# Reordering a branch's channels so that its passes through DRAM are wide transfers, and spreading the first loads over three queues

## The chip, the cores and the metric

One Trainium2 chip, all eight NeuronCores. Each core computes one sequence of the batch and the cores exchange nothing. The metric is the device time of the slowest core in microseconds (us). In some executions, of any kernel, one die (cores 0 to 3 or 4 to 7) or both show a lower granted TensorE clock and take longer; such runs are left out.

## The reference, cut to what matters

```python
D_MODEL, BATCH, SEQ, N_META = 2048, 8, 2048, 16       # 16 meta tokens in front: L = 2064
E_CONV = E_SSM = 1024; CONV_WIDTH = 31; SSM_GROUP = 16; SSM_STATE = 64

def reference(x, meta, norm_g, w_in, ...):
    h = jnp.concatenate([broadcast(meta), x], axis=1)
    xn = _rmsnorm(h, norm_g)
    proj = jnp.einsum("bld,de->ble", xn, w_in)         # v, g, z_c, u, z_s: 1024 columns each;
    v_c, g_c, z_c, u_s, z_s, gl_c, gl_s = split(proj)  # gl_c, gl_s: 2048 each
    y_c = _conformer_conv(v_c, g_c, z_c, ...)   # v*sigmoid(g), causal conv over 31 frames, LN, silu, *silu(z)
    y_s = gelu(_s5_scan(u_s, ...))              # diagonal state space, 64 groups of 16 channels
    y_s = y_s * sigmoid(y_s @ w_glu + b_glu)
    y_s = y_s * silu(z_s)
    merged = sigmoid(gl_c + b) * (y_c @ w_conv) + sigmoid(gl_s + b) * (y_s @ w_ssm)
    h = h + merged @ w_out
    return _rmsnorm(h, final_g)[:, N_META:, :]          # float32, (8, 2048, 2048)
```

## The kernel before

The kernel is a list of operations (each with engine, estimated duration, what it reads and writes, and a priority). A planner, written in Python and run when the kernel is built, simulates the five engines and the DMA and fixes **one order of instructions for each engine**. On the chip every engine runs its list in that order and waits on semaphores, whatever is ready behind. The planner's model of a DMA is this:

```python
    def schedule(self, bw=280e3):                 # bytes per us
        # ... cut: always take the ready operation of highest priority on the engine that is free first
            if o.dsrc is not None:                # a DMA: all share one pipe of 280 GB/s
                start = max(end, dma_free)
                dma_free = start + o.nbytes / bw
                end = dma_free + 2.2
            else:
                end += 0.2
            self.order[e].append(o)
```

Time is split in 8 phases j of NC = 258 frames. The input comes transposed in four quarters for each phase, all on the SP queue. It is squared and summed (ACT, DVE), summed over partitions by PE, normalised by square root and reciprocal, and scaled into XM, the right-hand operand of all projections:

```python
        def x_load(j):
            for q in range(4):
                t, b = XQ[j % 3][q]                                   # three chunk buffers of 4 quarters
                xl[j, q] = dma("sp", [(t, x_t[j][:, q * 4 * NC:(q + 1) * 4 * NC])], ..., prio=1)
        def x_chunk(j):
            # ... cut: Square, adds, matmul with ones
            act(r_, ps[bk][:, 0:NC], AF.Sqrt, bias=NORM_EPS, scale=1.0 / D, ...)
            xrc[j] = recip(r_, r_, NC, (rB,), (rB,), prio=2)
            # ... cut: 16 scalings into XM
```

Then come the u projections, 1024 matmuls of 258 columns, in waves as chunks arrive. Each result is copied by ACT to one of six small buffers ("pieces") and stored to DRAM. The scratch tensor is there because the state-space part needs another layout: PE produces 128 channels on the partitions, the scan wants partition = (phase j, channel h of its group) and the 8 groups g side by side. Before the change the DRAM tensor keeps a whole row of 2064 frames for each channel:

```python
    u_scr = scratch("u_scr", [8, 128, L])                             # row of 4128 bytes per channel
            cp("act", pt[:, 0:NC], ps[bk][:, 0:NC], ...)              # PSUM -> piece
            dma("sp", [(u_scr[m][:, lo:lo + NC], pt[:, 0:NC])], ...)  # 128 rows of 516 bytes, 4128 bytes apart
            # ... later, in the state-space part:
            us = u_scr[m].rearrange("(g h) (j c) -> j h g c", h=16, j=8)
            dma("sp", [(u3[16 * j:16 * j + 16, :, :], us[j]) for j in range(8)], ...)   # 8 narrow loads
```

The tensor a (v times sigmoid of g, on its way to the convolution), y (scan output) and c (convolution output) go the same way. The v and g projections that follow u run over five tiles of 412 or 414 columns (V_TILES).

## Time and profile before

| | before |
|---|---|
| time, median of 3 (lowest to highest) | 1682.75 us (1682.45 to 1683.12) |
| span by core in the profiled run | 1671.1 to 1683.8 us |
| PE work at full clock, a core with a complete record | 1609.7 us |
| PE time lost, mean of six cores | 56.2 us, 55.5 of it in the first 225 us |
| last quarter of the input lands | 106 to 114 us |
| last u matmul starts | 184 to 191 us |

The page of the profile, slowest core: the span, the busy tenths of PE in 40 slices of 42 us, the granted TensorE clock in tenths, the DMA packets, and the shares of the chain of waits that ended last.

```profile
span 1683.8 us, 23977 instructions; the slowest of 8 cores (1671.1 to 1683.8 us)
...
PE   3689899999999999999999999999999999999997
...
PEclk6899999999999999999999999999999999999999
...
DMA packets 129572, 200.70 MB, mean 119 GB/s; under 512 B 22576, under 2 KB 85296, under 8 KB 127280
...
PE 90%; DMA 5%; DVE 3%; issue 2%; ACT 0%; SPq 0%; DVEq 0%; ACTq 0%; POOL 0%; POOLq 0%
```

PE is full from the sixth slice on, at full clock. Only the first slices, and a little the fifth, have room.

The PE timeline of the same core: start, duration, line, operation, count; in brackets the idle time before it and what ended it. L605 is the matmul that sums a chunk's squares, L343 a projection.

```profile
26.94 2.06 PE L605 MATMUL ps<-CY,ST 128*128 128x258 f32 x4 [16.98 <-DVE CY L317]
34.55 1.02 PE L343 MATMUL ps<-XM,WS 128*128 128x258 bf16 x4 [5.56 <-DVE XM L328]
...
182.75 7.20 PE L343 MATMUL ps<-XM,WS 128*128 128x258 bf16 x64
189.79 5.76 PE L343 MATMUL ps<-XM,ST 128*128 128x414 bf16 x32
199.99 20.32 PE L343 MATMUL ps<-XM,ST 128*128 128x414 bf16 x101 [4.43 <-ACT ST L333]
```

The first projection stands at 34.55 us, the last 64 u matmuls end at 189.8 us, and after 32 more matmuls PE waits 4.43 us for a copy out of PSUM.

Waits of PE, from the table of waits (total us, times, longest):

```profile
PE ps L605 <- DVE CY L317: 25.0, 3, 17.0
...
PE ps L343 <- DVE XM L328: 12.0, 5, 5.6
PE ps L343 <- ACT ST L333: 10.8, 8, 4.4
```

### The profile page before, as it was taken

How to read it: one execution, taken by the hardware profiler on the slowest of the kernel's cores; microseconds unless marked ns; L12 is line 12 of the kernel's file. 1: busy time of each engine (PE TensorE's matmuls, PEld its weight loads, DVE VectorE, ACT ScalarE, POOL GpSimd, SP SyncE). 2: the span in 40 equal slices, each digit the busy share in tenths (PEclk: the TensorE clock that was granted, in tenths of full speed). 3: DMA queues.
4: the chain of work that ended last, by engine and by line, in shares of the span. 5: the costliest groups of instructions: out<-in, count | busy, mean ns of one | idle time of the engine just before them, and what ended most of it. 6: DMA issues, size and time to landing. Idle time of an engine off the chain costs nothing.

```text
span 1683.8 us, 23977 instructions; the slowest of 8 cores (1671.1 to 1683.8 us)
## 1 busy us (share of the span) xinstructions
PE 1615.7 (96%) x8565; PEld 841.5 (50%) x8650; DVE 725.3 (43%) x1254; ACT 522.5 (31%) x890; POOL 108.0 (6%) x220
## 2 busy tenths in 40 slices
PE   3689899999999999999999999999999999999997
PEld 2568666666655544444444444444444444444443
DVE  4978327867656826267322111111111122225433
ACT  2645214445345589344111111111111111122221
POOL 1000100000000000001010000000101100100000
PEclk6899999999999999999999999999999999999999
DMA  9972856777767873325764444445655653936612
GB/s 217 208 153 56 128 109 115 129 132 140 128 118 143 189 219 76 88 82 105 147 105 76 76 76 75 76 76 88 99 89 89 101 91 84 179 108 235 215 76 75
DMA packets 129572, 200.70 MB, mean 119 GB/s; under 512 B 22576, under 2 KB 85296, under 8 KB 127280
## 3 DMA queue, kind: packets, MB, share of 16 engines
q0 software_dynamic: 33792, 92.29, 35.8%
q1 hardware_dynamic: 95664, 106.88, 23.5%
q8 instruction: 71, 1.16, 0.3%
q14 instruction: 45, 0.37, 0.1%
HBM read 248.89 MB, written 42.50 MB: 173 GB/s over the span
## 4 chain that ended last, share of the span: by engine, by line
PE 90%; DMA 5%; DVE 3%; issue 2%; ACT 0%; SPq 0%; DVEq 0%; ACTq 0%; POOL 0%; POOLq 0%
PE ps L343 89%; DMA u_scr<-ST 2%; DVE CY L317 1%; DMA SM<-par 1%; DMA WS<-w_dw 1%; DMA CY<-x_t 1%; DVE XM L328 1%; PE ps L605 0%; DMA CY<-par_b 0%; SPq L355 0%; DVE ST L337 0%; DVE CY L328 0%; PE ps L349 0%; ACT ST L333 0%; PE ps L344 0%
## 5 line engine op out<-in xcount | busy, mean ns | idle before, releaser
L343 PE MATMUL ps<-XM,WS 128*128 128x512 bf16 (+3 forms) x5216 | 1013.4, 351 | 18.4 <-DVE XM L328 12.0
L343 PEld LDWEIGHTS ps<-XM,WS 128*128 128x128 bf16 x5216 | 511.3, 98 | 471.5 <-issue 24.1
L310 ACT ACTIVATE ST<-ps,SM 128x512 f32<-128x512 f32 (+2 forms) x224 | 135.7, 625 | 620.7 <-PE ps L343 589.7
L328 DVE SCALAR_TENSOR_TENSOR ST<-ps,ST 128x512 f32<-128x512 f32 x132 | 91.2, 691 | 507.1 <-PE ps L343 498.0
L343 PE MATMUL ps<-CY,WS 128*128 128x512 bf16 x1218 | 282.0, 379 | 3.3
L343 PEld LDWEIGHTS ps<-CY,WS 128*128 128x128 bf16 x1280 | 125.2, 98 | 151.0
L317 DVE TENSOR_TENSOR CY<-CY 128x257 f32<-128x257 f32 (+3 forms) x192 | 125.5, 669 | 31.5 <-ACT CY L310 14.2
L310 ACT ACTIVATE ST<-ps 128x512 bf16<-128x512 f32 (+3 forms) x112 | 61.2, 551 | 180.0 <-PE ps L343 176.8
L310 ACT ACTIVATE CY<-CY 128x514 f32<-128x514 f32 (+2 forms) x104 | 87.7, 861 | 66.5 <-DVE CY L317 30.4
L317 DVE TENSOR_TENSOR CY<-ps,CY 128x514 f32<-128x514 f32 (+1 forms) x96 | 65.1, 685 | 93.4 <-PE ps L343 88.9
L355 POOL DMA_DIRECT2D WS<-w_main x102 | 54.3, 532 | 594.8 <-PE ps L343 546.6
L343 PE MATMUL ps<-XM,ST 128*128 128x512 bf16 (+2 forms) x411 | 85.9, 371 | 4.7 <-ACT ST L333 4.4
L317 DVE TENSOR_TENSOR CY<-CY,ST 128x128 f32<-128x128 f32 (+3 forms) x112 | 62.2, 590 | 39.1 <-DMA CY<-par_b 19.4
L317 DVE TENSOR_TENSOR ST<-ST 128x512 f32<-128x512 f32 (+3 forms) x87 | 55.0, 647 | 33.5 <-ACT ST L947 28.7
L343 PEld LDWEIGHTS ps<-XM,ST 128*128 128x128 bf16 x416 | 41.4, 100 | 48.8 <-issue 7.7
L333 ACT CAST ST<-ps 128x258 bf16<-128x258 f32 (+1 forms) x96 | 41.4, 442 | 70.4 <-PE ps L343 56.2
L343 PE MATMUL ps<-XM 128*128 128x512 bf16 x251 | 56.3, 379 | 0.3
L343 PE MATMUL ps<-CY,XM 128*128 128x512 bf16 x251 | 56.3, 379 | 0.3
L343 PE MATMUL ps<-CY,ST 128*128 128x512 bf16 x251 | 55.2, 379 | 0.3
L328 DVE SCALAR_TENSOR_TENSOR XM<-CY,SM,ST 128x258 bf16<-128x258 f32 x128 | 51.6, 480 | 0.3
L343 PE MATMUL ps<-CY 128*128 128x256 bf16 (+1 forms) x320 | 50.6, 272 | 0.0
L328 DVE SCALAR_TENSOR_TENSOR ST<-ST,ps 128x412 bf16<-128x412 f32 (+1 forms) x40 | 23.3, 584 | 60.6 <-PE ps L343 39.3
(81 smaller groups left out, 809.2 us busy)
## 6 DMA issues: line engine op xcount, KB each, us to landing
WS<-w_main POOLq DMA_DIRECT2D x102, 512.0 KB, 8.2
CY<-x_t SPq DMA_DIRECT2D x32, 516.0 KB, 13.2
WS<-w_br POOLq DMA_DIRECT2D x32, 512.0 KB, 6.7
WS<-w_dw POOLq DMA_DIRECT2D x32, 320.0 KB, 7.2
z_scr<-ST SPq DMA_DIRECT2D x64, 128.0 KB, 3.9
ST<-z_scr SPq DMA_DIRECT2D x32, 256.0 KB, 3.4
WS<-x SPq DMA_DIRECT2D x8, 1024.0 KB, 6.9
CY<-x SPq DMA_DIRECT2D x8, 1024.0 KB, 12.8
```

What stands on the lines that cost most here:

```text
L310: f = lambda e: e.activation(out=out_, in_=in_, func=func, bias=bias, scale=scale)
L317: return S.op(eng, lambda e: e.tensor_tensor(out=out_, in0=in0, in1=in1, op=op), d, reads, writes, **kw)
L328: return S.op("dve", lambda e: e.scalar_tensor_tensor(out=out_, in0=in0, scalar=scalar, in1=in1, op0=op0, op1=op1), 0.15 + n / 960.0, read ...
L333: return S.op("act", lambda e: e.copy(out=out_, in_=in_), 0.22 + n / 1200.0, reads, writes, **kw)
L343: return lambda e: e.matmul(a[0], a[1], a[2], start=a[3], stop=a[4])
L355: return lambda e: e.dma_start(out=o, in_=i, allow_slow_non_contiguous=True)
```

## The change

The intent: permute the channels of each group of 128 on the host (weights, biases), so that the wanted layout in DRAM has long runs, and each of the eight narrow transfers per tile becomes one transfer with rows of 4 KB on one side; start earlier by loading the first chunk over two queues, weights and later chunks over a third; replace square root and reciprocal with Ln and Exp on ACT. The diff also changes the planner's DMA model and makes the v, g and convolution weight loads wait for an earlier tile.

```diff
-    def schedule(self, bw=280e3):
+    def schedule(self, bw=320e3):
-                start = max(end, dma_free)
-                dma_free = start + o.nbytes / bw
-                end = dma_free + 2.2
+                now, left = max(end, ring[e]), float(o.nbytes)
+                others = sorted(v for q, v in ring.items() if q != e and v > now)
+                while True:                      # each queue its own pipe; they share 320 GB/s
+                    rate = min(bw / (1 + len(others)), 0.78 * bw)
+                    # ... cut
+                ring[e] = end = now + left / rate
+                end += 2.2
# ... cut
-    u_scr = scratch("u_scr", [8, 128, L])
-    a_scr = scratch("a_scr", [8, 128, L])
-    y_scr = scratch("y_scr", [8, 128, SEQ])
-    c_scr = scratch("c_scr", [8, 128, SEQ])
+    u_scr = scratch("u_scr", [8, 8, 128, NC])
+    a_scr = scratch("a_scr", [8, 8, 128, NC + 2])
+    y_scr = scratch("y_scr", [8, 8, 128, NR])
+    c_scr = scratch("c_scr", [8, 8, 128, NR])
# ... cut: the input loads
+                eng = ("act" if q % 2 else "sp") if j == 0 else "sp" if j < 3 else "pool"
+                xl[j, q] = dma(eng, [(t, x_t[j][:, q * 4 * NC:(q + 1) * 4 * NC])], ...,
+                               prio=0 if j == 0 else 1 + j / 10, after=...)
# ... cut: the power tables of the scan move behind chunk 3; the small parameters load later
-            act(r_, ps[bk][:, 0:NC], AF.Sqrt, bias=NORM_EPS, scale=1.0 / D, ...)
-            xrc[j] = recip(r_, r_, NC, (rB,), (rB,), prio=2)
+            act(r_, ps[bk][:, 0:NC], AF.Ln, bias=NORM_EPS, scale=1.0 / D, ...)
+            xsq[j] = act(r_, r_, AF.Exp, scale=-0.5, ...)
# ... cut: v and g in 8 tiles of 258 (5 of 412 before), eleven piece buffers of 520 bytes (6 of 1024)
-            pi, pt, pB = piece()
-            dma("sp", [(u_scr[m][:, lo:lo + NC], pt[:, 0:NC])], ...)
+            pi, pt, pB = chunk_piece()
+            dma("sp", [(u_scr[m][j], pt[:, 2:NC + 2])], ...)      # 128 rows of 516 bytes, touching
# ... cut
-            us = u_scr[m].rearrange("(g h) (j c) -> j h g c", h=16, j=8)
-            dma("sp", [(u3[16 * j:16 * j + 16, :, :], us[j]) for j in range(8)], ...)
+            dma("sp", [(u2, u_scr[m].rearrange("j (h g) c -> (j h) (g c)", g=8))], ...)
# ... cut: a the same; y and c one wide store each, and a narrow read in one issue
# ... cut: the swap of halves by matmul becomes two ACT copies
+    sw = np.arange(E).reshape(8, 8, 16).transpose(0, 2, 1).reshape(-1)     # on the host
+    for a in range(0, 5 * E, E):
+        w_in[:, a:a + E] = w_in[:, a + sw]
+    w_conv, w_ssm, w_glu = p["w_conv"][sw], p["w_ssm"][sw], p["w_glu"][sw][:, sw]
```

## The prediction

> **What bounds it now.** TensorE: the page gives PE 96% busy, the chain of waits is 90% PE. By stage (table of windows, slowest core) it is 98-100% busy at granted clock 1.00 from 210 us to its last matmul at 1673 us. Only the first 200 us have room: PE 13.5, 29.2 and 35.4 us busy in the first three 42 us windows, clock 0.67, 0.80, 0.92. In the PE timeline the first projection stands at 34.6 us; the first 1024 matmuls (128x258, 110.8 ns each back to back: 208 in 23.04 us) end at 189.8 us, for 113.5 us of work. Then comes a 4.4 us wait for a copy out of PSUM (behind a store of narrow pieces, 16.6 us in the chain) and a cold restart (128 matmuls in 25.0 us, 174 ns each when warm: 2.7 us lost). The warm times of all matmuls after 200 us leave under 8 us of loss there, plus a 10 us tail. So relief of DMA, SP, DVE or ACT after 200 us is worth nothing.
>
> **What the change does.**
> 1. Wide transfers: u and a reads go from 1024 packets of 516 B (28 ns each) to 128 of 4128 B (160 ns), 1.8 to 1.3 us per tile on 16 engines, and 7 of 8 issues vanish (0.4-0.5 us of SP each). For y and c the narrow side only moves from write to read. All under a saturated PE: about 0.
> 2. Start. The first chunk's loads get two queues, and no competition from three early weight loads and later chunks. The Trainium skill (DMA: Bandwidth & Descriptors, Issuing engines are not separate DMA queues) says that more queues save only issue time; I count the ordering, not bandwidth. The small parameter load now lands at 24 us (20.5 us in the chain), holding DVE; afterwards earlier. Estimate from 300 GB/s seen here: first projection near 22 us.
> 3. Chunk chain: the reciprocal (1.77 us, DVE, x8) becomes Ln and Exp on ACT (about 0.4 each; the skill's ScalarE: Activation LUTs, Table sets, has both in one set, so no 1.28 us reload per chunk). DVE, 40.5 of 42 us busy from 42 to 84 us, then needs 10.6 us per chunk, not 12.4; the power tables (about 9 us) move behind chunk 3. Chunks come every 12 us, not 14-15.
> 4. Eleven piece buffers for six: most waits for copies (10.8 us in the table of waits) go.
> 5. PE work: v/g tiles of 258 for 412: 2048x110.8 - 1280x174.1 ns = +4.1 us. Swap matmuls to ACT: 16x0.215 = -3.4 us.
>
> **Sum.** Steps 2-4: projections end near 153 us, not 190: -37. Gap and cold restart: -7. PE work: +0.7. Narrow tiles with three banks leave 3.5 us, not 5.6, for emptying a bank: +3 of new stalls. About -40 us: **1643 us**, range 1627 to 1663. Chances: faster by over 2% 0.62, within 2% 0.37, slower 0.01.
>
> **What would show it.** First projection at 20-26 us; last u matmul at 145-162 us; no 4 us gap after; no table load between Ln and Exp; PE still 99-100% from 210 us; some 11,000 DMA packets fewer without effect after 200 us.
>
> **What would make it wrong.** Loads of chunks 3-7 stuck behind weight loads on the POOL queue; all cores loading at once, chunks slower than 12 us; table reloads per chunk (+2.6 us each); the static instruction order, planned with faster DMA, making PE wait in order; narrow v/g tiles stalling over 5 us; or the start shrinking more than I think (limit about -60 us).

## More of the kernel before

Kernels are compared by executions in the undisturbed state.

Near the middle comes the gate stage: 32 gate matmuls, then the two branch matmuls of 8 each, for 64 blocks. The second branch, the state-space one, needs YS already multiplied by z, in 16 multiplications on DVE, the z tiles coming back from DRAM through three buffers:

```python
            if n % 2:
                for m in range(8):
                    z_, zB = z_load(m, h, 4)                          # 128x1024, from DRAM, 3 buffers
                    tt(ys, ys, z_, ALU.mult, n=1024, ...)
        # ... gate stage, for each block: gates, then
                    for br_, (sv, sB) in enumerate(((CBv, CBq), (YSv, YSq))):
                        proj(b3[:, br_ * 8:br_ * 8 + 8, :], brB, 0, lambda k: sv[:, k, n * 512:(n + 1) * 512], ...)
```

"PE time lost" is my own sum over the trace: for each matmul, the time from its start to the next matmul's start, less what a matmul of that width takes when nothing holds it. For that I use columns / 2.4 + 2.5 ns, which fits the distance of starts that the trace shows back to back (110 ns at 258 columns, 174 ns at 412, 216 ns at 512, core 1); a matmul of 4-byte numbers counts four times. The sum counts waits and the cold clock after them. Two of the eight cores miss some 85 matmul records in each trace and are left out.

The gate stage in the PE timeline of core 1 (whose matmul records are complete):

```profile
788.97 7.07 PE L343 MATMUL ps<-XM,WS 128*128 128x512 bf16 x32
795.88 1.89 PE L343 MATMUL ps<-CY,WS 128*128 128x512 bf16 x8
...
806.24 7.07 PE L343 MATMUL ps<-XM,WS 128*128 128x512 bf16 x32
813.14 7.07 PE L343 MATMUL ps<-CY,WS 128*128 128x512 bf16 x32
```

The last matmul of the preceding stage (GLU) starts at 788.8 us. PE then runs three blocks of 32 gate matmuls with two conv products between them before it comes to the state-space products at 813.14, 24.4 us later. The last of the DVE multiplications they need (the ninth in DVE's list, eight for this half and one for the next) had ended at 808.5 us, 19.7 us after that GLU matmul:

```profile
807.82 0.69 DVE L317 TENSOR_TENSOR CY<-CY,ST 128x1024 bf16<-128x1024 bf16 x1 [2.80 <-DMA ST<-z_scr]
```

The order planned has some 5 us to spare here, and nothing waits.

## The result

The changed kernel is correct and takes 1703.7 us in the median of 4 runs (1701.48 to 1705.5), against 1682.93 us (1682.45 to 1684.09) for the kernel before. The ratio is 1.0122 with a 95% interval of 1.0104 to 1.0139: 1.2% slower, where 2.4% faster was predicted. A ratio here is always the mean time of one kernel's fast runs over that of the other's fast runs of the same rounds, so not quite the ratio of the medians quoted. The calls ran on several chips, and the kernel before took 1682.9 to 1686.5 us in them, so between calls 2 or 3 us mean nothing.

The page after, the same lines:

```profile
span 1701.6 us, 25563 instructions; the slowest of 8 cores (1688.3 to 1701.6 us)
...
PE   4789999999999999997999999999999999999997
...
PEclk7899999999999999998999999999999999999999
...
DMA packets 115114, 200.85 MB, mean 118 GB/s; under 512 B 19376, under 2 KB 68784, under 8 KB 112816
...
PE 85%; DMA 10%; DVE 2%; ACT 1%; issue 1%; SPq 1%; POOL 0%; DVEq 0%; ACTq 0%; POOLq 0%
```

Packets fell by 14,458 (129,572 to 115,114). The DMA share of the chain rose from 5% to 10%, and slice 19 (766 to 808 us), where PE was full before, falls to 7 with the clock at 8.

The PE timeline of the slowest core (L619 sums squares, L350 is a projection):

```profile
20.82 2.06 PE L619 MATMUL ps<-CY,ST 128*128 128x258 f32 x4 [10.76 <-DVE CY L324]
25.80 1.02 PE L350 MATMUL ps<-XM,WS 128*128 128x258 bf16 x4 [2.92 <-DVE XM L335]
...
173.31 7.21 PE L350 MATMUL ps<-XM,WS 128*128 128x258 bf16 x64
180.37 3.68 PE L350 MATMUL ps<-XM,ST 128*128 128x258 bf16 x32
185.96 0.61 PE L356 MATMUL ps<-ident,CY 128*128 128x128 bf16 x8 [1.91 <-DVE CY L324]
```

The start came as predicted: the first projection at 25.80 us for 34.55, and no 4 us gap when u ends. But the last 64 u matmuls start at 173.3 us and end at 180.4 us, 10 us earlier than before, not 37.

The waits of PE:

```profile
PE ps L350 <- DVE CY L324: 16.0, 1, 16.0
...
PE ps L350 <- ACT ST L340: 13.3, 5, 4.5
...
PE ps L619 <- DVE CY L324: 10.8, 1, 10.8
...
PE ps L350 <- DVE XM L335: 9.2, 2, 6.3
```

Waits for copies (ACT, L340) did not go; they are 13.3 us, where they were 10.8. And there is a wait of 16 us that did not exist before. It stands in the gate stage, here on core 1:

```profile
785.69 7.07 PE L350 MATMUL ps<-XM,WS 128*128 128x512 bf16 x32
792.60 1.89 PE L350 MATMUL ps<-CY,WS 128*128 128x512 bf16 x8
810.84 3.55 PE L350 MATMUL ps<-CY,WS 128*128 128x512 bf16 x8 [16.35 <-DVE CY L324]
```

After the first block, PE goes straight from the conv product at 792.60 to the state-space product, and stands idle for 16.35 us until DVE has the last of the multiplications done, at 810.7 us (the first of the two in this line):

```profile
810.00 1.29 DVE L324 TENSOR_TENSOR CY<-CY,ST 128x1024 bf16<-128x1024 bf16 x2 [3.74 <-DMA ST<-z_scr]
```

GLU's last matmul starts at 785.5, so that is 25.2 us later, where it was 19.7 us before; and PE now asks for it 9 us after that GLU matmul, not 24. The idle time here is 12.4 to 16.4 us on every core, and the clock is cold afterwards.

Where the time went, as PE loss by stage, mean of six cores (us):

| kernel | to 225 us | 225 to 500 | 500 to 740 | 740 to 900 | sum | mean span of those cores |
|---|---|---|---|---|---|---|
| before | 55.5 | 0.5 | 0.2 | 0.0 | 56.2 | 1679.1 |
| after | 49.1 | 2.2 | 5.7 | 17.3 | 74.3 | 1696.7 |

PE's own work changed from 1609.7 to 1608.2 us. So the sum is -6.4 (start), +7.2 (middle), +17.3 (gate stage), -1.5 (work): +16.6 us, for +17.6 us in span. Two questions follow. Where does the gate stage's 17 us come from? And why did the start give 6 us, of some 44 expected?

### The profile page after: what moved, and what is told of

Read it like the earlier page. It is cut to its first block, busy times and chain, and to the rows that moved or that the text cites. A ratio compares the mean times of both kernels' runs of the same rounds, so it can differ in the third digit from the quotient of the medians.

```text
span 1701.6 us, 25563 instructions; the slowest of 8 cores (1688.3 to 1701.6 us)
## 1 busy us (share of the span) xinstructions
PE 1623.4 (95%) x9402; PEld 917.5 (54%) x9402; DVE 714.3 (42%) x1265; ACT 532.5 (31%) x926; POOL 117.4 (7%) x226
## 2 busy tenths in 40 slices
DMA packets 115114, 200.85 MB, mean 118 GB/s; under 512 B 19376, under 2 KB 68784, under 8 KB 112816
## 4 chain that ended last, share of the span: by engine, by line
PE 85%; DMA 10%; DVE 2%; ACT 1%; issue 1%; SPq 1%; POOL 0%; DVEq 0%; ACTq 0%; POOLq 0%
PE ps L350 85%; DMA CY<-x_t 3%; DMA ST<-z_scr 2%; DMA u_scr<-ST 2%; DVE CY L324 1%; DMA SM<-par 1%; SPq L362 1%; DMA CY<-c_scr 1%; DMA CY<-par_b 1%; ACT ST L317 1%; DMA a_scr<-ST 1%; ACT L317 0%; DVE XM L335 0%; PE ps L619 0%; ACT CY L317 0%
## 5 line engine op out<-in xcount | busy, mean ns | idle before, releaser
L350 PE MATMUL ps<-XM,WS 128*128 128x512 bf16 (+1 forms) x5888 | 1020.7, 331 | 27.5 <-ACT ST L340 13.3
L350 PEld LDWEIGHTS ps<-XM,WS 128*128 128x128 bf16 x5888 | 578.6, 99 | 428.1 <-issue 34.8
L350 PE MATMUL ps<-CY,WS 128*128 128x512 bf16 x1280 | 288.9, 381 | 16.0 <-DVE CY L324 16.0
L350 PEld LDWEIGHTS ps<-CY,WS 128*128 128x128 bf16 x1280 | 125.5, 98 | 168.2 <-issue 18.2
L317 ACT ACTIVATE ST<-ps 128x258 f32<-128x258 f32 (+1 forms) x136 | 65.2, 485 | 186.8 <-PE ps L350 184.6
L317 ACT ACTIVATE CY<-CY 128x514 f32<-128x514 f32 (+3 forms) x112 | 96.5, 875 | 69.6 <-DMA CY<-x_t 34.4
L350 PE MATMUL ps<-XM,ST 128*128 128x258 bf16 (+1 forms) x512 | 83.9, 326 | 0.0
L350 PEld LDWEIGHTS ps<-XM,ST 128*128 128x128 bf16 x512 | 50.0, 98 | 33.4
L340 ACT CAST ST<-ps 128x258 bf16<-128x258 f32 (+1 forms) x96 | 42.0, 440 | 57.4 <-PE ps L350 42.6
L350 PE MATMUL ps<-CY,XM 128*128 128x512 bf16 x256 | 56.6, 379 | 0.0
L350 PE MATMUL ps<-XM 128*128 128x512 bf16 x256 | 56.6, 379 | 0.0
L350 PE MATMUL ps<-CY,ST 128*128 128x512 bf16 x256 | 55.4, 379 | 0.0
L335 DVE SCALAR_TENSOR_TENSOR ST<-ST,ps 128x258 bf16<-128x258 f32 x64 | 27.0, 422 | 66.5 <-PE ps L350 54.1
L350 PE MATMUL ps<-CY 128*128 128x256 bf16 (+1 forms) x320 | 52.4, 272 | 0.0
```

What stands on the lines that cost most here:

```text
L317: f = lambda e: e.activation(out=out_, in_=in_, func=func, bias=bias, scale=scale)
L335: return S.op("dve", lambda e: e.scalar_tensor_tensor(out=out_, in0=in0, scalar=scalar, in1=in1, op0=op0, op1=op1), 0.15 + n / 960.0, read ...
L340: return S.op("act", lambda e: e.copy(out=out_, in_=in_), 0.22 + n / 1200.0, reads, writes, **kw)
L350: return lambda e: e.matmul(a[0], a[1], a[2], start=a[3], stop=a[4])
```

## The experiments

Theory at this point: the gate stage wait comes from the planner's new DMA model, not from the data layout. For the start, the supply of input and weights bounds it, not the DVE chain. Rivals: the layout causes the gate wait; the chain of squares bounds the start. All kernels were correct but two.

### 1. The planner's model: f110_old_plan, f001_new_plan, plan220

f110_old_plan is the changed kernel with the old model of `schedule`:

```diff
-    def schedule(self, bw=320e3):           # and the model of three rings
+    def schedule(self, bw=280e3):           # and the model of one pipe
```

> The kernel after, but the instruction order is planned with the old DMA model (one shared 280 GB/s pipe). Theory P (planning): the 16 us PE wait near 790 us exists only because the new, faster DMA model placed the first SSM-branch matmuls ahead of data that DVE finishes at 805-811 us; with the old model the order leaves slack, the wait near 790 us falls under 3 us and the time to 1682-1690 us. Rival L (layout): the narrow reads of c and y make the data itself late; then the wait stays over 8 us and the time stays 1695-1706 us.

Measured: 1686.92 us (1684.99 to 1690.56), before 1684.54 in the same rounds, ratio 1.0017 [0.9999, 1.0035]. The wait in the gate stage is gone; on core 1:

```profile
778.05 7.07 PE L342 MATMUL ps<-XM,WS 128*128 128x512 bf16 x32
...
795.32 7.07 PE L342 MATMUL ps<-XM,WS 128*128 128x512 bf16 x32
802.23 7.07 PE L342 MATMUL ps<-CY,WS 128*128 128x512 bf16 x32
```

Now PE again runs three gate blocks ahead, and the state-space product at 802.23 waits for nothing: its last multiplication had ended at 797.8 us, 20.0 us after the last GLU matmul. The reverse, f001_new_plan, is the kernel before with the new model only.

> The kernel before, only the planning model new. Theory P: a PE wait of 8-18 us appears at the first SSM-branch matmuls (780-800 us), time 1692-1702 us. Rival L: no such wait, time 1680-1686 us.

Measured: of four runs two had a slow die (1782 and 1912 us); the two others took 1703.2 and 1705.7 us, so no interval is given. In the profiled run every core waits 7 to 11 us from 794 to 804 us on, here core 7:

```profile
813.44 3.29 PE L351 MATMUL ps<-CY,WS 128*128 128x512 bf16 x8 [11.06 <-DVE CY L325]
```

The model alone costs 17 us in the changed kernel (1703.7 against 1686.9) and some 20 us in the kernel before (1703.2 and 1705.7 against 1684.5, a little over the 1692 to 1702 expected). There only 12.1 us are lost in the gate stage; another 5.0 are added to the loss at the start, where the first projection now stands at 40 to 42 us. The model is a cause, and independent of the layout.

plan220 asks whether still more caution helps: the changed kernel with the old model at 220 GB/s.

> The kernel after, planned with the old one-pipe DMA model at 220 instead of 280 GB/s: more slack in the static order than with the old plan. If slack is what the waits of PE after 200 us lack (some 8-15 us are left on most cores with the old plan), 1676-1684 us; if they are late data that no order of this kind helps, 1684-1692 us; over 1692 us if the pessimistic plan delays the start.

Measured: 1688.46 us, ratio 1.0013 [0.9995, 1.0030]. Loss falls to 1.7 us in the middle, rises by 8.8 us at the start against f110_old_plan, and 2.9 us are lost in the gate stage. More caution in this number wins nothing.

### 2. Is it PE's order alone? margin20, margin_first

In the trace of core 1, z loads issued between 777 and 793 us take 9 to 13 us to land before and 10 to 16 after, while weights stream; before, one issued at 782.2 landed at 795.0. I wanted to give the changed kernel slack back by telling the planner that the state-space products become ready later.

```diff
-  proj(b3[:, br_ * 8:br_ * 8 + 8, :], ..., bk, nk=8, halves=1)
+  proj(b3[:, br_ * 8:br_ * 8 + 8, :], ..., bk, nk=8, halves=1, margin=20.0 * br_)
```

> The kernel after; in the gate stage alone the SSM-branch matmuls are planned as if their data came 20 us later, so that PE does other gate matmuls first. All data, transfers and the plan up to there stay. Theory P (planned too early, data itself not late enough to matter): the wait of 12-16 us near 790 us and its cold restart go, 1684-1691 us. Rival L (the data of this stage is late in any order): the wait moves but stays over 8 us, 1695-1706 us.

Measured: 1745.41 us, ratio 1.0338 [1.0315, 1.0362]. A miss: a margin in all 64 blocks made the planner leave small gaps everywhere (27.7 us of loss after 900 us, where the others have none), and 13.7 us are still lost in the gate stage. The lever was too coarse. margin_first gives 14 us to the first column block only.

> The kernel after; only for the first output block of the gate stage the SSM-branch matmuls are planned 14 us later, so that PE first does the gate matmuls of the next block (the earlier try shifted every block by 20 us and put planned gaps into all of them). Theory P: the one wait of 12-16 us near 790 us shrinks to under 4 us, nothing else changes, 1686-1693 us. Rival L: a wait of over 8 us stays, 1696-1706 us.

Measured: 1709.23 us, ratio 1.0151 [1.0135, 1.0167]. A miss again, but one that teaches; the PE timeline of core 1:

```profile
784.82 7.07 PE L350 MATMUL ps<-XM,WS 128*128 128x512 bf16 x32
...
802.09 5.34 PE L350 MATMUL ps<-XM,WS 128*128 128x512 bf16 x24
807.53 3.61 PE L350 MATMUL ps<-CY,WS 128*128 128x512 bf16 x16
...
827.06 3.54 PE L350 MATMUL ps<-CY,WS 128*128 128x512 bf16 x8 [12.47 <-DVE ST L335]
```

PE now has two gate blocks ahead, and the first state-space products at 807.53 come just when their multiplication ends (807.4 us). But 7 us later PE stops and waits 12.47 us all the same, now for a step of DVE that merges two branches. The chain of waits on this core leads back from it to the DVE list: the merge stands behind multiplications for the second half, and those wait for their z tiles, the last of which landed at 825.5 us. So the wait moved from one list to another. Not only PE's order but DVE's as well was planned for z tiles that come sooner than they do; the mean loss in this stage is 15.5 us, 17.3 without the margin. To have the margin help, both lists would have to change together, which is what the old model does.

### 3. The parts alone: f100_start, f010_layout

f100_start is the kernel before with the new start only (queues, order of loads, Ln and Exp, the power tables later). f010_layout is the kernel before with the new layout only (channel order, scratch tensors, tiles of 258, eleven pieces). Both have the old planner model.

> The kernel before with only the new start (loads on three queues in a fixed succession, parameters early, Ln and Exp for square root and reciprocal, power tables after chunk 3), old layout and old planning. If the start is worth what the two traces show, 8-14 us: time 1669-1675 us. If the start's gain came from the layout's eleven piece buffers, under 4 us: 1679-1684 us.

Measured: 1684.96 us, ratio 1.0003 [0.9988, 1.0018], above both ranges expected. The last u matmul comes 10 us earlier (175 to 180 us), but a single wait of 10 to 13 us follows at 187 to 203 us: DVE cannot write v times g, because a piece is still being stored (24.5 us from issue to landing).

> The kernel before with only the new layout (channels reordered, wide transfers, 258-wide v/g tiles, eleven piece buffers, swap on ACT), old start and old planning. Theory P: within 6 us of before, 1678-1690 us, with a wait of some 4 us at the first read of the narrow c pieces (570-620 us). Rival L: 1693-1702 us with the long wait near 790 us.

Measured: 1689.89 us, ratio 1.0034 [1.0015, 1.0052]. The layout alone, with all its wide transfers, is a little slower. And one thing does not fit: its last quarter of x lands at 122 to 130 us (before: 106 to 114). The input loads themselves are the same in the two kernels.

### 4. What bounds the start? x_half, chain_light

Both are made from the changed kernel and give a wrong result. x_half loads half of each quarter for chunks 3 to 7:

```diff
-  dma(eng, [(t, x_t[j][:, q * 4 * NC:(q + 1) * 4 * NC])], ...)
+  w = 4 if j < 3 else 2
+  dma(eng, [(t[:, 0:w * NC], x_t[j][:, q * 4 * NC:(q * 4 + w) * NC])], ...)
```

> The kernel after; chunks 3 to 7 load only half their columns (the rest is left from an older chunk: wrong result on purpose), 5.3 MB less, same instructions in the same order. Theory D (the start is bound by the delivery of inputs by DMA, x and weights together some 230-240 GB/s): chunk 7's statistics matmul comes at 120-132 us instead of 146 us and the last u matmul at 162-172 us instead of 179 us. Rival C (bound by each chunk's own chain on ACT, DVE and PE): both move less than 4 us.

chain_light squares and adds a quarter of the columns:

```diff
-  act(s_, t, AF.Square, ...);            tt(part, part, s_, ALU.add, ...)
+  act(s_[:, 0:NC], t[:, 0:NC], ...);     tt(part[:, 0:NC], part[:, 0:NC], s_[:, 0:NC], ...)   # for q > 0
```

> The kernel after; three of four squares and the three adds of each chunk work on a quarter of the columns (wrong result on purpose), which takes 2.4 us of DVE and 1.9 us of ACT from each chunk, same loads and order. Theory D: chunk 7's statistics matmul stays within 6 us of 146 us and the last u matmul within 5 us of 179 us. Rival C: they come 15-20 us and 10 us or more earlier.

Measured: x_half 1703.28 us, ratio 1.0097 [1.0073, 1.0120]; last u matmul at 164 to 176 us, up to 10 us earlier than in the changed kernel. chain_light 1720.61 us, ratio 1.0200 [1.0178, 1.0221]; last u matmul at 176 to 188 us, no earlier. (Two fast runs each.) In the changed kernel, then, the chain of squares does not bound the u stage, which refutes the rival there. Theory D is met in part only: chunk 7's statistics matmul comes at 130 to 142 us in x_half, not 120 to 132 (138 to 146 in the changed kernel), so halving the loads of five chunks bought a few us; and in chain_light, with the same loads, it comes at 142 to 154 us and the kernel takes 17 us longer than the changed one, which I cannot explain. No gain of the start reached the end in x_half: the waits in the middle and the gate stage (17.7 us) stay.

### 5. Which piece of the layout is slow? u_wide, u_wide11, c_write

u_wide is f100_start with the channels reordered and u alone in the new form (block store, one wide read); a, y and c stay narrow. u_wide11 has eleven pieces for u as well.

> The kernel before with the new start and the old planning (as the run of the start alone, 1685 us), plus one part of the layout: channels reordered and the u read as one wide transfer; a, y and c stay narrow as before, v/g tiles stay 412 wide, six piece buffers. Theory T: the start alone lost its 12 us again in one wait of 10-12 us at 185-200 us, because the eight narrow u loads held SyncE's queue for 16 us in front of the stores that free the piece buffers; with wide u loads the wait falls under 5 us and the time to 1674-1680 us. If the wait has another cause it stays and the time is 1683-1688 us.

> The same with eleven piece buffers for the u pieces. If piece buffers are what PE waits for in the u stage, 2-6 us under the previous run; if input delivery is, within 2 us of it.

Measured: u_wide 1710.39 us, ratio 1.0158 [1.0140, 1.0176]; last u matmul at 190 to 196 us, then the wait of 10 to 20 us as in f100_start. u_wide11 1696.87 us, ratio 1.0087 [1.0048, 1.0126]; 8 to 15 us of wait are left on most cores (the profiled run, 1707 us, is the slowest of the four). I had expected u_wide to gain. Making one tensor's transfers wide cost some 25 us against f100_start.

c_write is f110_old_plan with c narrow on the write and wide on the read, to test whether the narrow read of c makes the waits near 580 us.

> The kernel after with the old planning (1687 us), and c alone with its narrow side back on the write and a wide read. Theory N: the waits of some 3-5 us at 570-610 us come from the narrow reads of c, which the layer norm waits for; they fall under 1.5 us, 1681-1685 us. Rival: the waits stay (c itself is late), 1685-1690 us.

Measured: 1685.80 us, ratio 1.0013 [0.9995, 1.0031]. Loss between 500 and 740 us is 3.9 us, 4.2 without the edit. The narrow read is not the main cause; what is stays open.

### 6. The address of a store: u_contig, u_pad1k

Across kernels the pattern was plain by now. Whenever u was stored in blocks of touching 516-byte rows, the last input quarter landed at 118 us or later (f010_layout, f110_old_plan, after, u_wide, u_wide11); with rows 4128 bytes apart it landed at 105 to 114 us (before, f100_start). Only f001_new_plan blurs this, with rows 4128 bytes apart, a later start and 115 to 120 us. On core 1 f100_start and f110_old_plan have the whole fourth chunk at 46.5 and 50.0 us and the fifth at 66.6 and 76.1; u stores begin at 30 us. The new theory: the **address** of the u stores slows the input loads. Rival: the order of instructions, the queues or the pieces. u_contig is f100_start with nothing but the address changed. It still has eight narrow reads, the old channel order, six pieces; every engine's list of instructions is the same, in the traces too.

```diff
-    u_scr = scratch("u_scr", [8, 128, L])
+    u_scr = scratch("u_scr", [8, 8, 128, 258])             # u_pad1k: 512 for 258
-            dma("sp", [(u_scr[m][:, lo:lo + NC], pt[:, 0:NC])], ...)
+            dma("sp", [(u_scr[m][j][:, 0:NC], pt[:, 0:NC])], ...)
-            us = u_scr[m].rearrange("(g h) (j c) -> j h g c", h=16, j=8)
+            us = u_scr[m].rearrange("j (g h) c -> j h g c", h=16)[:, :, :, 0:NC]
```

> The kernel of f100_start with one thing changed: each 128x258 tile of u is stored to DRAM as one block of 516-byte rows, one behind the other (as in the change), and read back with 8 narrow loads as before. The order of instructions on every engine is the same. Theory A (the address of the stores slows the input loads): the last quarter of chunk 7 lands at 118 to 127 us (f100_start 105 to 106), the median store of u takes 6 to 10 us to land (f100_start 3.3 to 3.9), the mean 4128-byte packet between 50 and 105 us takes 295 to 325 ns (f100_start 242 to 256), the last u matmul is at 184 to 193 us, the time 1690 to 1706 us. Rival B (order, queues and piece buffers of the layout do it, not the address): all as in f100_start, time 1685 within 3 us.

> As u_contig, but the rows of a block are 1024 bytes apart. Theory A1 (stores to rows that touch each other are slow, or share a line of memory): as f100_start, last input quarter at 104 to 108 us, time 1682 to 1688. Theory A2 (a compact block is slow wherever its rows begin): close to u_contig, last input quarter above 114 us, time above 1689. Rival B: the same as f100_start and as u_contig.

Measured: u_contig 1703.83 us (1702.77 to 1706.08), ratio 1.0109 [1.0092, 1.0127]. u_pad1k 1685.47 us, ratio 1.0000 [0.9982, 1.0017]. The last input quarter lands at 121 to 124 us in u_contig and at 103 to 109 us in u_pad1k (f100_start: 105 to 109); the last u matmul starts at 190 to 194 and at 174 to 181 us. Eighteen microseconds from nothing but the address of a scratch tensor's rows.

How does the profile show it? These are lines from the DMA view between 60 and 110 us: all packets; packets, MB and share of 16 engines' time of the software queue (it carries the input and weight loads); the input loads with the median time from issue to landing. First f100_start:

```profile
DMA packets 5485, 10.65 MB, mean 213 GB/s; under 512 B 626, under 2 KB 3238, under 8 KB 5480
...
q0 software_dynamic: 2532, 9.24, 80.8%
...
CY<-x_t POOLq DMA_DIRECT2D x11, 516.0 KB, 15.3
```

Then u_contig:

```profile
DMA packets 4088, 9.14 MB, mean 183 GB/s; under 512 B 454, under 2 KB 2078, under 8 KB 4085
...
q0 software_dynamic: 2256, 8.27, 92.8%
...
CY<-x_t POOLq DMA_DIRECT2D x11, 516.0 KB, 21.9
```

Then u_pad1k:

```profile
DMA packets 5099, 10.26 MB, mean 205 GB/s; under 512 B 584, under 2 KB 2909, under 8 KB 5095
...
q0 software_dynamic: 2469, 9.01, 79.1%
...
CY<-x_t POOLq DMA_DIRECT2D x11, 516.0 KB, 16.3
```

In 50 us the software queue moved 9.24, 8.27 and 9.01 MB and occupied the engines for 80.8, 92.8 and 79.1% of their time. Divided (bytes / (share x 50 us x 16)) an engine moved 14.3, 11.1 and 14.2 GB/s while it worked on such a packet. A 4128-byte input packet that began between 50 and 105 us took 242 to 256 ns in the mean of a core in f100_start, 304 to 318 in u_contig and 235 to 256 in u_pad1k, with the median at 160 in all three. The store packets themselves show nothing: 516 bytes took 30 to 32 ns in the mean in all of them. So a reader who looks at the store packets finds them innocent; the reads beside them pay, in a longer tail. From issue to landing the stores pay as well: in this stretch their median is 13.6 to 16.6 us by core in u_contig, against 8.1 to 12.7 in f100_start (over the whole kernel 4.9 to 6.5, mostly under the 6 to 10 expected, against 3.0 to 4.5). How much of the 18 us comes through the late input and how much through pieces that come free late, the runs do not separate.

What about touching rows does it is not settled. It is not the compact block alone, since u_pad1k writes within 128 KB and is fast, and not an odd start alone, since the rows before began at 4128 x channel + 516 x phase bytes. What is left is that two stores meet inside one piece of memory, or that odd starts and small distances come together; no run tells these apart. Nor does a run tell whether a core is slowed by its own stores or by a neighbour's.

### 7. The cure in the changed kernel: f110_pad, f100_pool

f110_pad is f110_old_plan with u rows 1024 bytes apart. The read becomes 1024 packets of 516 bytes again, in one issue.

```diff
-    u_scr = scratch("u_scr", [8, 8, 128, NC])
+    u_scr = scratch("u_scr", [8, 8, 128, 512])
-            dma("sp", [(u2, u_scr[m].rearrange("j (h g) c -> (j h) (g c)", g=8))], ...)
+            dma("sp", [(u3, u_scr[m].rearrange("j (h g) c -> (j h) g c", g=8)[:, :, 0:NC])], ...)
```

> The changed kernel with the old planning model (f110_old_plan, 1686.9), the u rows in DRAM 1024 bytes apart, read with one transfer of 516-byte packets. Theory A1: last input quarter at 104 to 110 us instead of 122 to 125, last u matmul at 165 to 172 us instead of 179 to 180, time 1674 to 1681, the first version ahead of both kernels. A2: 1684 to 1688. Rival B: 1687 within 2 us.

Measured: 1670.13 us (1669.13 to 1676.35), before 1686.06, ratio 0.9918 [0.9887, 0.9949]. It is 17 us faster than f110_old_plan, and the first kernel ahead of both. The loss to 225 us is 35.1 us, 49.1 without the edit, and the long wait at the end of u is down to 3.5 us.

f100_pool moved the narrow u loads of f100_start from SP to POOL, because SP was 16 us busy issuing eight of them ahead of a store:

> f100_start with the narrow loads of u issued by the POOL queue instead of SP (the planned order changes a little with it). Theory C (SP, blocked for 16 us by 8 narrow loads, holds back the stores that free the piece buffers): the wait of 10 to 12 us near 187 to 202 us falls below 3 us, time 1673 to 1679. Rival D (the stores themselves are slow there, whoever issues the loads): the wait stays above 7 us, time 1683 to 1687.

Measured: 1686.12 us, ratio 1.0003 [0.9986, 1.0021]. The wait is still there, 12.3 us on the slowest core: the store in question was issued at 176.0 us and landed 26.7 us later. The blocked queue was not the cause, so this theory falls. u_pad1k has that wait too (13.9 us), f110_pad does not; f110_pad also has eleven pieces, for u and a, and one issue for each read. Which of these removes it was not isolated.

### 8. Do the causes add up? after_pad, pad_ua

after_pad is the changed kernel as it was, new planner model included, with the u rows apart as in f110_pad.

> The changed kernel as it is, new planning model included, with only the u rows in DRAM 1024 bytes apart and one read of 516-byte packets. The order of instructions on PE, DVE, ACT and POOL is the changed kernel's. If the two causes add up: the last u matmul at 165 to 172 us instead of 178 to 180, the single wait of 12 to 17 us in the gate stage stays (now near 775 to 785 us), time 1684 to 1691. If the gate wait comes from the late start in some way, it shrinks below 8 us and the time is under 1680. If the address matters only with the old plan, the time stays above 1697.

Measured: 1690.56 us, ratio 1.0043 [1.0023, 1.0064], at the upper edge of what was expected for adding up. The last u matmul is at 160 to 164 us. The gate stage wait is untouched, on core 7:

```profile
798.07 3.57 PE L350 MATMUL ps<-CY,WS 128*128 128x512 bf16 x8 [14.52 <-DVE CY L324]
```

pad_ua is f110_pad with the rows of a apart as well:

```diff
-    a_scr = scratch("a_scr", [8, 8, 128, NC + 2])
+    a_scr = scratch("a_scr", [8, 8, 128, 512])                  # and store and read of rows [0:NC + 2]
```

> f110_pad with the rows of a, the gated tensor that the convolution reads, also 1024 bytes apart instead of 520 (one read of 520-byte packets). Order of instructions the same. If compact rows hurt there too: the loss between 200 and 300 us (1 to 6 us a core, a wait of 3.3 us at 272 us on cores 1 and 5 behind an a store that took 6.1 us) falls below 2 us, time 1665 to 1669. If PE at work hides it: 1670 within 2 us. Reading 520-byte packets for one wide packet may add a wait: then up to 1674.

Measured: **1665.14 us** in the median (1664.07 to 1665.96, three fast runs), before 1684.66, ratio 0.9890 [0.9871, 0.9910]. It is 1.1% faster than the kernel before and the best version found. Its gain over f110_pad is not certain, since the two intervals overlap; the loss to 500 us fell from 40.0 to 31.2 us. Its page:

```profile
span 1662.4 us, 25554 instructions; the slowest of 8 cores (1650.5 to 1662.4 us)
...
PE   4899999999999999999999999999999999999997
...
PE 92%; DMA 3%; DVE 2%; SPq 1%; ACT 1%; issue 1%; ACTq 0%; DVEq 0%; POOLq 0%
```

The loss by stage, mean of six cores, of the kernels that carry the argument:

| kernel | u rows | planner | to 225 us | 225 to 500 | 500 to 740 | 740 to 900 | sum | median time |
|---|---|---|---|---|---|---|---|---|
| f100_start | apart | old | 54.8 | 0.6 | 1.0 | 0.0 | 56.4 | 1684.96 |
| u_contig | touching | old | 74.0 | 0.9 | 0.1 | 0.0 | 75.0 | 1703.83 |
| u_pad1k | apart | old | 55.5 | -0.1 | 0.1 | 0.0 | 55.5 | 1685.47 |
| after | touching | new | 49.1 | 2.2 | 5.7 | 17.3 | 74.3 | 1703.7 |
| f110_old_plan | touching | old | 49.1 | 3.3 | 4.2 | 0.0 | 56.6 | 1686.92 |
| after_pad | apart | new | 34.4 | 2.6 | 6.1 | 16.9 | 60.0 | 1690.56 |
| f110_pad | apart | old | 35.1 | 4.9 | 3.4 | 0.0 | 43.4 | 1670.13 |
| pad_ua | apart, a too | old | 29.9 | 1.3 | 4.2 | 0.0 | 35.4 | 1665.14 |

Read the changed kernel as two switches: touching rows cost about 14 to 15 us at the start in either plan, the new planner model about 17 us in the gate stage with either address. In these sums they do not interact; in the times the planner is worth 17 us with touching rows and 20 with rows apart, which across chips is no clear difference.

What bounds the start once the rows are apart? The table of windows, for 80 to 160 us, in the changed kernel (core 6) and in pad_ua (core 5); the first figure after the comma is PE's busy time in us, the third from the end the granted clock:

```profile
80.00:160.00 80.00, 70.48 (x582) 59.42 (x583) 58.81 (x126) 46.15 (x82) 4.21 (x8) 0.94 0.61 120
80.00:160.00 80.00, 79.98 (x720) 70.17 (x719) 74.01 (x161) 48.95 (x91) 4.24 (x8) 1.00 0.49 118
```

In pad_ua PE is full from 80 us on, on every core, and between 20 and 130 us ACT waits 0 to 6.6 us for input, where it waited 19 to 29 us in the changed kernel. So there the supply of input no longer bounds the end of u. Some 11 to 14 us are lost before 20 us and 18 to 23 between 20 and 80; what holds PE in that stretch no run isolates.

## Why the prediction was wrong, point by point

- **"Steps 2-4: projections end near 153 us, not 190: -37"** is the first failed term. The last u matmul came at 172 to 180 us, some 10 us earlier than before, and the loss to 225 us fell by 6.4 us. Two errors are in it. One is below, the address. The other is the estimate "Chunks come every 12 us": the matmuls that sum the squares of chunks 0 and 7 lie 125 us apart on core 6 after (20.8 to 146.2), 17.9 us a chunk, and still 14.6 us in pad_ua (21.0 to 123.5, core 5), where the rows of u and a are apart. I took the DVE chain for the bound; in the changed kernel chain_light shows that it was not, and the waits for input (19 to 29 us on ACT) point to the supply. Even with the address cured, u ended at 160 to 172 us, not 153; there PE is full from 80 us on in pad_ua, so what was mis-sized is the stretch before, and its cause stays open.
- **Step 1, "Wide transfers ... All under a saturated PE: about 0"**, is the second, and the one that I would not have found by adding up durations. The step costed the reads and the issues, which did prove worthless: 14,458 packets fewer with no gain. It did not ask where the **stores** now go. They run while PE is still hungry for input, and their new addresses cost the input loads over a fifth of their rate: 14 to 15 us of loss in the changed kernel, 18 us of time with the address alone (u_contig).
- **"PE still 99-100% from 210 us"** is the third, and as large: 17.3 us in the gate stage. "The static instruction order, planned with faster DMA, making PE wait in order" was named among the things that could go wrong, and got no weight in the sum or the chances. One planner constant and one model in the diff decided it (f110_old_plan, f001_new_plan).
- **"+3 of new stalls"** was 7.2 us between 225 and 740 us, and "most waits for copies (10.8 us in the table of waits) go" was 13.3 us instead. In pad_ua the table of waits has 1.2 us for a copy. So the eleven pieces do their work once stores land fast; that this is the reason is argued, not isolated.
- Right: the first projection at 20 to 26 us (24.4 to 25.8 by core); no 4 us gap when u ends (1.91 us); PE's work nearly unchanged (+0.7 predicted, -1.5 in my sum, where a matmul of 258 columns counts 110.0 ns and not 110.8); no table load between Ln and Exp of a chunk (27 table loads in all after, 32 before). The skill has both functions in one set (ScalarE: Activation LUTs, Table sets: the hidden batching unit), and the trace agrees.
- Nearly right, from the skill's DMA: Bandwidth & Descriptors (Issuing engines are not separate DMA queues): three queues save issue time alone. In the first two slices of 42 us the page shows 217 and 208 GB/s before, 234 and 183 after: over the two no rate was gained. But f100_start, with the new start and the old rows, moved 231 GB/s in its first 84 us, mean of the cores, where before moved 213. So the new start did bring 8% more bytes, and the touching rows took them again; whether the queues, the earlier issue or the order did it was not isolated.

## What to carry to other kernels

When a change moves data to another place in DRAM, ask what runs beside the **stores**, and look at the reads for the harm: here rows of 516 bytes that touched cost other transfers over a fifth of their rate, and padding them to 1024 bytes bought back 13 to 18 us. A planner's DMA constant is part of the kernel: test it alone, because a static order without slack turns one late load into a stop of the busiest engine. And to find such a cause, build two kernels whose instruction lists are equal and differ in one address; no view of a single profile pointed to it here.

## What the Trainium skill lacked or had wrong

- DMA: Bandwidth & Descriptors says that transfers reach full rate from 512 bytes on, below which there is a read-modify-write (Specifications). The rows here were 516 bytes and took 30 to 32 ns in the mean either way, but touching rows slowed the loads beside them from 14.3 to 11.1 GB/s per engine (f100_start, u_contig). The page has nothing on stores that slow other transfers.
- The same page (Latency and other measured facts, the row on HBM row pitch) advises, at large powers of two (512 KiB to 8 MiB), to pad the pitch by a few KiB "or lay tiles out contiguously". For the small rows here, a case that it does not treat, the contiguous layout was the slow one (1703.83 us) and rows 1024 or 4128 bytes apart the fast ones (1685.47 and 1684.96 us).
- TensorE: Matmul & The Clock Gate (Part 1) says to budget, on the default power profile, a clock of 13/16 for dense matmuls on all cores, because a limiter takes a die there within 5 to 20 us of its third busy core. Most executions here ran dense matmuls on all eight cores at a mean granted clock of 0.98. The runs set aside as slow had a die whose mean was 0.81 to 0.96, so something like this comes in some executions only, which the page does not say.
- No page gives the time of a small load beside a burst of weight loads: z loads of 256 KB took 9 to 13 us to land while eight weight loads streamed, where the median of all z transfers of the kernel, stores included, is 3.6 us (core 1 before).
